# A hybrid decoder layer on one core: raw branch gates passed through the sigmoid at the merge, attention results loaded ahead, a new split of the fillers

## The chip, the cores and the metric

The kernel runs on one core of a Trainium2 chip. A core has a matrix engine (PE, which loads weights beside its matmuls, PEld), a vector engine (DVE), an activation engine (ACT), a general engine (POOL) and a queue engine (SP), which here issues all transfers between device memory and the on-chip buffers. Each engine works through its own instructions in order and waits for the others by semaphores. The metric is device time in microseconds, the median of several executions. Trace times are counted from the start of the profiled execution.

## The reference

One layer over 1024 positions of width 1024, in float32:

```
proj = rmsnorm(x) @ w_in        -> attention q,k,v, short-conv B,C,v, DeltaNet q,k,v,
                                   beta, decay, output gate z, and 3 x 1024 branch gates
A: forgetting attention (causal, 8 heads)                  -> y_fox
B: y_sc = B * causal_dwconv3(C * v)
C: gated delta rule in chunks, per-head RMSNorm * silu(z)  -> y_dn
merged = sum_b sigmoid(gate_b) * (y_b @ W_branch_b)
x = x + merged @ w_o
x = x + (silu(u_gate) * u_val) @ w_down   with u = causal_dwconv3(rmsnorm(x) @ w_up)
x = x + sigmoid(rmsnorm(x) @ w_pg) * (p @ w_ple)
```

The reference's delta rule has chunks of 64; the kernel works on 8 chunks of 128 with 4 heads side by side. In each chunk a lower triangular matrix A is built from k, beta and the decay, its inverse is formed, and a recursion over the chunks carries a state.

## The kernel before

Activations lie transposed, 128 channels by 1024 positions; `NB` are the two halves of 512 positions. Every float32 matmul is made of three: `split` (L127 to L130) writes a rounded high part on ACT (L129) and the rest as a low part on DVE or POOL (L130), and `step` multiplies high by high, high by low and low by high. A unit of the first projection is 128 output channels: 2 halves x 8 x 3 = 48 matmuls of 128x512 (`dense`). The normalised input is held in 16 tiles xg (8 high, 8 low), which the first projection reads until its last unit and which later operands reuse. Weights come in tiles wr of 512 KB and are split into wo.

Stages in order of time: the first norm and attention with projections in between (to about 522 us); phase f2, the delta rule, in two parts: the solve (`dn_solve`: building A, inverting 32x32 blocks on DVE, completing them to 128x128 on PE) and the steps (`dn_prep`, `dn_state`, `dn_out` for 8 chunks); then phase la with the gates, the merge, w_o, the channel mixer and the last projection.

The units of the first projection that nothing needs at once are fillers for PE. There are 32 of them: 12 for the short convolution, 4 for z, and 16 raw gates of branches 0 and 2 (the gates of branch 1 are made later, in phase la). `PLAN` says how many are started at which point of attention, solve and steps; a filler's result goes unscaled to device memory (`raw_tile`, L503 and L504, 64 stores of 256 KB). Within the plan the order of all instructions on each engine is set by the scheduler, which runs a timeline of its own.

In the solve, `decay` loads per chunk a row tile gb (256 KB, L703), DVE makes et of it (4 instructions, L705), ACT the exponential; a tile kc (256 KB, L717) is multiplied by itself on PE, and DVE writes A (L722). gb and kc have 2 buffers each. With all eight chunks of A, DVE transposes (L728), does the forward substitution in 31 rounds (L734, L736), and transposes back to TT (L739) and X (L748); then PE's first product with X (`to64`) can start. The recursion's tail is `dn_out` of the last chunk: products into po, squares on ACT, small steps on DVE, a scaling (L859), and transposes on PE (L862).

In phase la, eight units make the gates of branch 1, each followed by `gate` for two tiles of a raw gate (branches 0 and 2): load from device memory, product with the norm's scale rs on DVE (`mul`, L950), sigmoid on ACT (L986), store (L987). Four short convolutions (`short_conv`) and four output gatings (`dn_gated`) on DVE and ACT follow units 0 to 3 and 4 to 7; each keeps 1024 positions in tiles yr (4 buffers) and stores its y. At the merge, per branch, four y tiles are loaded (`load`, into yr), split into xg, and eight units of 24 matmuls are multiplied by the gates, which come back through tiles sg (4 buffers). Branch 0 writes `merged`, 1 and 2 add to it on POOL (L1021).

Of the kernel before, what the change touches and what calls it, by code (L numbers as in the profile page):

```python
# [7 lines left out]
F32 = mybir.dt.float32  # L8
# [5 lines left out]
P = 128  # L14
# [13 lines left out]
WR, WO, SUMS, SUBS = 2, 5, "gvgv", "vvvvvvg"  # L28
PLAIN = 2
MM, PQ, SM1, SM2 = 2, 2, 2, 4  # L30
PLAN = {"start": "krr", "tail": "rr", "solve": "rrrrrrrrrrr",
        "steps": ["rr", "rr", "r", "r", "r", "r", "r", "rr", "r"],
        "fox": [["", "", "", "v"],
                ["k", "v", "", ""],
                ["", "", "", "r"],
# [13 lines left out]
def hybrid_block(ctx: ExitStack, tc: tile.TileContext, I, out, dbg=None):  # L49
# [33 lines left out]
    def pt(tag, bufs, w=512, dt=F32):  # L83
        pool, n = homes.setdefault(tag, (scopes[-1], bufs))
        return pool.tile([P, w], dt, tag=tag, name=nm(tag), bufs=n)
# [14 lines left out]
    def tmp(role="tmp", dt=F32, w=512):  # L100
        return pt(role if role in homes else "tmp", 0, 516, dt)[:, 0:w]
# [597 lines left out]

    def decay(c, mask, op, sign):  # L700

        gb, e = pt("gb", 2), pt("et", 2)
        Q.dma_start(chunk(gb), cdr[8:12, hs(c)].partition_broadcast(P))  # L703
        for h in range(4):
            V.scalar_tensor_tensor(out=e[:, hs(h)], in0=gb[:, hs(h)], scalar=Gc[:, h, c : c + 1], in1=mask,  # L705
                                   op0=ALU.subtract, op1=op)
        S.activation(e, e, AF.Exp, scale=sign)
        return gb, e

    def dn_solve():  # L710
# [2 lines left out]
            G.memset(TT[:, 4 * c : 4 * c + 4, :], 0.0)  # L713
        for c in range(8):
            _, ee = decay(c, maskS, ALU.max, -1.0)
            kc = pt("kc", 2)
            Q.dma_start(chunk(kc), kdr[:, :, hs(c)])  # L717
            ps = smb()
            for h in range(4):
                mm(ps[:, hs(h)], kc[:, hs(h)], kc[:, hs(h)], True, True)  # L720
            for h in range(4):
                V.scalar_tensor_tensor(out=A[:, 4 * c + h, :], in0=ps[:, hs(h)], scalar=beta[:, h, c : c + 1],  # L722
                                       in1=ee[:, hs(h)], op0=ALU.mult, op1=ALU.mult)
# [220 lines left out]
    with phase("la", psum=dict(mm=6, sm=2), a=16, wq=3):  # L944
        with phase("me", tmp=9, sg=4, yr=4):
# [3 lines left out]
            def mul(o, x, y):  # L949
                V.tensor_tensor(out=o, in0=x, in1=y, op=ALU.mult)  # L950
# [27 lines left out]
                mul(y, y, z)  # L978
                Q.dma_start(ydr[2][j], y)

            def gate(b, dt, nb, ps):
                g = tmp()
                if ps is None:
                    Q.dma_start(g, raw[U_GT + 8 * b + dt][:, NB[nb]])
                mul(g, g if ps is None else ps, rs[:, NB[nb]])
                S.activation(g, g, AF.Sigmoid)  # L986
                Q.dma_start(gdr[b, dt][:, NB[nb]], g)  # L987

            for b in range(3):
                for dt in range(8):  # L990
                    gdr[b, dt] = dr.tile([P, T], F32, tag=f"g{b}{dt}", name=f"g{b}{dt}")
            for dt in range(8):
                dense(wload(I["win"][U_GT + 8 + dt]), KT, xg, lambda nb, ps, dt=dt: gate(1, dt, nb, ps))
                for i in range(2):
                    for nb in range(2):
                        gate(2 * (dt // 4), 2 * (dt % 4) + i, nb, None)
                (short_conv, dn_gated)[dt // 4](dt % 4)

            merged = [big() for _ in range(8)]
            for b in range(3):  # L1000
                ys = []
                for j in range(4):
                    y, h, l = load(ydr[b][j]), xgt(), xgt()
                    split(h, l, y)
                    ys.append((h, l))
                for d2 in range(4):
                    sgs = {}
                    for dt in (2 * d2, 2 * d2 + 1):
                        for nb in range(2):
                            sgs[dt, nb] = pt("sg", 4)  # L1010
                            Q.dma_start(sgs[dt, nb], gdr[b, dt][:, NB[nb]])
                    w = wload(I["wbr"][4 * b + d2])
                    for dt in (2 * d2, 2 * d2 + 1):
                        def ev_b(nb, ps, dt=dt):
# [243 lines left out]
```

## Time and profile before

| what | value |
|---|---|
| median of three executions | 2026.06 us (2025.57 to 2030.67) |
| the profiled execution, its time | 2031.17 us |
| its span in the trace | 2029.4 us |
| PE busy | 1946.1 us, 96% |
| DVE, ACT, POOL busy | 1336.6, 906.9, 534.5 us |
| mean granted clock of PE | 0.985 |
| moved by transfers | 236.2 MB, mean 116 GB/s |

The page's second part cuts the span into 40 slices of 50.7 us; a digit is the busy share in tenths. The queries of waits give for each pair of waiting line and releasing line the sum, the number of times and the longest wait. A row of stretches gives the busy time of each engine, the granted clock, the share in which the DMA engines were busy, and GB/s. In rows of groups the idle time stands after the bar, with what ended it. On PE the durations of single matmuls overlap, so the pace is read from how many start in a stretch.

### The profile page before, as it was taken

What the parts mean: (1) busy time and instruction counts of PE and PEld (TensorE: products, weight loads), DVE (VectorE), ACT (ScalarE), POOL (GpSimd) and SP (SyncE); (2) the same over time, 40 slices, a digit from 0 to 9 for tenths busy, and PEclk for the clock granted to TensorE, in tenths of its full rate; (3) what the DMA queues carried; (4) which work ended last, traced back from release to release, by engine and by line L of the source; (5) the groups of instructions that cost most, each with busy time, mean ns of one, the idle gap of its engine ahead of it and who ended that gap; (6) DMA issues with size and microseconds to landing.
All of it is one profiled execution on the core that took longest, in us unless ns stands there. A gap on an engine that the chain in (4) does not pass through costs nothing. (4 is left out here: it accounts for less than half of the span.)

```text
span 2029.4 us, 25549 instructions
## 1 busy us (share of the span) xinstructions
PE 1946.1 (96%) x9281; PEld 1616.4 (80%) x9281; DVE 1336.6 (66%) x2157; ACT 906.9 (45%) x1651; POOL 534.5 (26%) x435
## 2 busy tenths in 40 slices
PE   8999999999997999999499999999999999999998
PEld 6788888888786888878388887787777778888887
DVE  6888788888396123348654537888788788544564
ACT  6576877677221233334421325544444444212351
POOL 1545334434322221200015310234334341000210
PEclk9999999999998999999699999999999999999999
DMA  4221122122431334259964523112221216432132
GB/s 174 69 97 58 57 68 80 47 82 77 146 101 51 99 122 131 90 206 395 366 220 136 191 96 123 62 52 83 73 94 63 94 63 237 137 94 73 52 109 89
DMA packets 111854, 236.20 MB, mean 116 GB/s; under 512 B 10384, under 2 KB 41456, under 8 KB 111728
## 3 DMA queue, kind: packets, MB, share of 16 engines
q1 hardware_dynamic: 111728, 234.57, 33.8%
q8 instruction: 73, 1.20, 0.2%
q14 instruction: 53, 0.43, 0.1%
HBM read 167.37 MB, written 67.16 MB: 116 GB/s over the span
## 5 line engine op out<-in xcount | busy, mean ns | idle before, releaser
L126 PE MATMUL mm<-xg,wo 128*128 128x512 f32 x6128 | 1493.6, 395 | 44.8 <-ACT xg L129 28.8
L126 PEld LDWEIGHTS mm<-xg,wo 128*128 128x128 f32 x6128 | 1146.4, 189 | 288.3 <-ACT xg L129 29.2
L126 PE MATMUL mm<-a,wo 128*128 128x512 f32 x1216 | 304.1, 390 | 0.3 <-ACT u L227 0.3
L129 ACT ACTIVATE wo<-wr 128x512 fp32r<-128x512 f32 x232 | 144.7, 626 | 292.8 <-PE mm L126 284.5
L126 PEld LDWEIGHTS mm<-a,wo 128*128 128x128 f32 x1216 | 229.0, 188 | 48.2 <-ACT u L227 0.7
L130 POOL TENSOR_TENSOR wo<-wr,wo 128x512 fp32r<-128x512 f32 x108 | 152.1, 1410 | 356.9 <-ACT wo L129 349.1
L1160 DVE TENSOR_TENSOR a<-mm,a 128x512 f32<-128x512 f32 x96 | 65.3, 690 | 92.1 <-PE mm L126 91.9
L130 DVE TENSOR_TENSOR wo<-wr,wo 128x512 fp32r<-128x512 f32 x124 | 96.2, 777 | 40.4 <-ACT wo L129 40.1
L1021 POOL TENSOR_TENSOR a<-a,sg 128x512 f32<-128x512 f32 x32 | 50.3, 1574 | 232.2 <-DMA sg<-g 197.3
L280 POOL TENSOR_TENSOR tmp<-tmp,tmp 128x512 f32<-128x512 f32 x21 | 27.7, 1323 | 286.9 <-ACT tmp L278 285.0
L130 DVE TENSOR_TENSOR wo<-wq,wo 128x512 fp32r<-128x512 f32 x68 | 79.2, 1166 | 3.4 <-ACT wo L129 3.4
L1073 DVE SCALAR_TENSOR_TENSOR o<-cw,cols,o 128x1024 f32<-128x1024 f32 x44 | 77.8, 1768 | 0.0
L491 DVE SCALAR_TENSOR_TENSOR o<-cv,cols,o 128x512 f32<-128x512 f32 x72 | 69.9, 971 | 10.1 <-ACT o L489 9.1
L129 ACT ACTIVATE wo<-ws 128x512 fp32r<-128x512 f32 x80 | 50.2, 631 | 56.5 <-PE mm L126 54.8
L503 ACT ACTIVATE o<-mm 128x512 f32<-128x512 f32 x60 | 35.7, 594 | 88.7 <-PE mm L126 70.4
L600 ACT ACTIVATE pp<-pp,small 128x512 f32<-128x512 f32 (+2 forms) x96 | 58.4, 610 | 27.9 <-DVE small L594 27.5
L1105 POOL TENSOR_TENSOR cg<-o,cg 128x1024 f32<-128x1024 f32 x22 | 55.0, 2501 | 48.1 <-ACT cg L1104 48.1
L199 POOL TENSOR_TENSOR ws<-wq 128x512 f32<-128x512 f32 x20 | 27.8, 1392 | 120.1 <-DMA wq<-wup 87.4
L130 DVE TENSOR_TENSOR pl<-pq,ph 128x512 fp32r<-128x512 f32 (+1 forms) x80 | 49.9, 629 | 13.9 <-ACT ph L129 13.5
L1071 ACT ACTIVATE o<-cw,cols 128x1024 f32<-128x1024 f32 x22 | 25.4, 1156 | 75.1 <-DVE cw L223 75.1
L199 POOL TENSOR_TENSOR ws<-wq,wq 128x512 f32<-128x512 f32 x20 | 43.7, 2184 | 56.3 <-DVE wo L130 52.3
L1073 DVE SCALAR_TENSOR_TENSOR o<-cg,cols,o 128x1024 f32<-128x1024 f32 x44 | 57.2, 1301 | 0.8 <-ACT o L1071 0.7
(289 smaller groups left out, 2407.2 us busy)
## 6 DMA issues: line engine op xcount, KB each, us to landing
wr<-win SPq DMA_DIRECT2D x64, 512.0 KB, 3.5
wq<-wup SPq DMA_DIRECT2D x44, 512.0 KB, 3.5
r<-o SPq DMA_DIRECT2D x64, 256.0 KB, 2.5
g<-tmp SPq DMA_DIRECT2D x48, 256.0 KB, 6.0
sg<-g SPq DMA_DIRECT2D x48, 256.0 KB, 2.9
ad<-o SPq DMA_DIRECT2D x20, 512.0 KB, 3.8
wq<-ad SPq DMA_DIRECT2D x20, 512.0 KB, 4.6
wr<-wdn SPq DMA_DIRECT2D x20, 512.0 KB, 3.6
```

Of the source, the lines that this page charges most:

```text
L126: pe[0] = nc.tensor.matmul(o, lhsT=l, rhs=r, start=start, stop=stop, skip_group_check=more)
L129: S.activation(h, x, AF.Copy)
L130: (eng or V).tensor_tensor(out=l, in0=x, in1=h.bitcast(F32), op=ALU.subtract)
L199: (G if e == "g" else V).tensor_tensor(out=o, in0=x, in1=y, op=op)
L280: eng[nb].tensor_tensor(out=acc[nb], in0=acc[nb], in1=sq, op=ALU.add)
L491: V.scalar_tensor_tensor(out=o, in0=cv[:, i : i + 512], scalar=col(c0 + i), in1=o, op0=ALU.mult, op1=ALU.add)
L503: S.activation(o, ps, AF.Copy)
L600: S.activation(t[:, :w], t[:, :w], AF.Exp, bias=mn[:, k - 1 : k], scale=-1.0, accum_out=sm[:, i : i + 1])
L1021: G.tensor_tensor(out=m, in0=m, in1=t, op=ALU.add)
L1073: V.scalar_tensor_tensor(out=o, in0=cv[:, i : i + T], scalar=col(c0 + i), in1=o, op0=ALU.mult, op1=ALU.add)
L1105: G.tensor_tensor(out=sg, in0=o, in1=sg, op=ALU.mult)
L1160: V.tensor_tensor(out=x2[dt][:, NB[nb]], in0=ps, in1=x2[dt][:, NB[nb]], op=ALU.add)
```

## The change

Six things are different.

- `PLAN`: the solve starts 13 fillers instead of 11; the steps start 2, 1, 1, 1, 1, 1, 1, 1, 1 instead of 2, 2, 1, 1, 1, 1, 1, 2, 1 (at the ninth point no filler is left, before as now).
- gb has 3 buffers instead of 2.
- kc has 4 buffers instead of 2.
- The raw gates of branches 0 and 2 no longer pass through device memory a second time. `gate` and its 32 loads and 32 stores are gone; the merge loads the raw gate into sg, multiplies it by rs on DVE and applies the sigmoid on ACT there. The gates of branch 1 are made as before.
- The four attention results are loaded at the start of phase la into four tiles of their own (fox), not at the merge into yr.
- The list of scaled gates in device memory shrinks from 24 to 8.

```diff
-PLAN = {"start": "krr", "tail": "rr", "solve": "rrrrrrrrrrr",
-        "steps": ["rr", "rr", "r", "r", "r", "r", "r", "rr", "r"],
+PLAN = {"start": "krr", "tail": "rr", "solve": "rrrrrrrrrrrrr",
+        "steps": ["rr", "r", "r", "r", "r", "r", "r", "r", "r"],
...
-        gb, e = pt("gb", 2), pt("et", 2)
+        gb, e = pt("gb", 3), pt("et", 2)
...
-            kc = pt("kc", 2)
+            kc = pt("kc", 4)
...
-            def gate(b, dt, nb, ps):
-                g = tmp()
-                if ps is None:
-                    Q.dma_start(g, raw[U_GT + 8 * b + dt][:, NB[nb]])
-                mul(g, g if ps is None else ps, rs[:, NB[nb]])
-                S.activation(g, g, AF.Sigmoid)
-                Q.dma_start(gdr[b, dt][:, NB[nb]], g)
-
-            for b in range(3):
-                for dt in range(8):
-                    gdr[b, dt] = dr.tile([P, T], F32, tag=f"g{b}{dt}", name=f"g{b}{dt}")
+            fox = [big() for _ in range(4)]
+            for j in range(4):
+                Q.dma_start(fox[j], ydr[0][j])
             for dt in range(8):
-                dense(wload(I["win"][U_GT + 8 + dt]), KT, xg, lambda nb, ps, dt=dt: gate(1, dt, nb, ps))
-                for i in range(2):
-                    for nb in range(2):
-                        gate(2 * (dt // 4), 2 * (dt % 4) + i, nb, None)
+                gdr[dt] = dr.tile([P, T], F32, tag=f"g{dt}", name=f"g{dt}")
+
+                def ev_g(nb, ps, dt=dt):
+                    g = tmp()
+                    mul(g, ps, rs[:, NB[nb]])
+                    S.activation(g, g, AF.Sigmoid)
+                    Q.dma_start(gdr[dt][:, NB[nb]], g)
+                dense(wload(I["win"][U_GT + 8 + dt]), KT, xg, ev_g)
                 (short_conv, dn_gated)[dt // 4](dt % 4)
...
-                    y, h, l = load(ydr[b][j]), xgt(), xgt()
+                    y, h, l = load(ydr[b][j]) if b else fox[j], xgt(), xgt()
...
-                            sgs[dt, nb] = pt("sg", 4)
-                            Q.dma_start(sgs[dt, nb], gdr[b, dt][:, NB[nb]])
+                            g = sgs[dt, nb] = pt("sg", 4)
+                            Q.dma_start(g, (gdr[dt] if b == 1 else raw[U_GT + 8 * b + dt])[:, NB[nb]])
+                            if b != 1:
+                                mul(g, g, rs[:, NB[nb]])
+                                S.activation(g, g, AF.Sigmoid)
```

The scheduler then orders the engines anew from the solve on. Three places matter. Names are those of the code, with numbers that tell tiles apart; L is the line, and the waits name the semaphores that an instruction waits for.

SP's queue in the building of A, before: the third gb waits for DVE, and the third and fourth kc wait for PE.

```order
L703 DMA gb_5646<-cdr 128x4x128 [waits DMAHW1_49]
L717 DMA kc_5654<-kdr 128x4x128 [waits DMAHW2_49,PE_49]
L703 DMA gb_5665<-cdr 128x4x128 [waits DMAHW6_49,DMAHW3_49,DVE_49]
L504 DMA r_6204<-o_6238 128x512 [waits DMAHW4_49,Activation_49]
L703 DMA gb_5684<-cdr 128x4x128 [waits DMAHW5_49,DMAHW1_49,DVE_49]
L717 DMA kc_5673<-kdr 128x4x128 [waits DMAHW7_49,PE_49]
L717 DMA kc_5692<-kdr 128x4x128 [waits DMAHW2_49,PE_49]
```

The same place now:

```order
L703 DMA gb_5646<-cdr 128x4x128 [waits DMAHW1_49]
L717 DMA kc_5654<-kdr 128x4x128 [waits DMAHW2_49]
L703 DMA gb_5665<-cdr 128x4x128 [waits DMAHW3_49]
L717 DMA kc_5673<-kdr 128x4x128 [waits DMAHW4_49]
L717 DMA kc_5692<-kdr 128x4x128 [waits DMAHW5_49]
L703 DMA gb_5684<-cdr 128x4x128 [waits DMAHW6_49,DVE_49]
L504 DMA r_6204<-o_6238 128x512 [waits DMAHW7_49,Activation_49]
```

The third gb and two more kc now follow at once; the fourth gb is the first that waits for DVE.

PE where the solve's first products with X stand (sm from X and A; mm are a filler's matmuls). This piece of the difference is from the stretch after the forward substitution:

```order
 L126 MATMUL mm_6668<-xg_245,wo_6665 128x512
+L126 MATMUL sm_5907<-X_5899,A_1235_5905 128x128 x4
+L126 MATMUL sm_5914<-sw_5897,TT_5618 128x128 x4
+L126 MATMUL sm_5915<-TT_5618,sw_5897 128x128 x4
 L126 MATMUL mm_6668<-xg_258,wo_6665 128x512
 L126 MATMUL mm_6668<-xg_259,wo_6665 128x512
-L126 MATMUL sm_5892<-X_5884,A_1231_5890 128x128 x4
```

The first product with X (sm_5892) has left this place for one 30 filler matmuls earlier, and the products of the second chunk stand where it was.

DVE where the merge begins, before (xg from yr: the attention results' low parts):

```order
L950 TENSOR_TENSOR tmp_9303<-tmp_9303,rs_427 128x512 [waits DMAHW4_49,DMAHW0_49]
L950 TENSOR_TENSOR tmp_9308<-tmp_9308,rs_427 128x512 [waits DMAHW7_49,DMAHW3_49]
L950 TENSOR_TENSOR tmp_9313<-tmp_9313,rs_427 128x512 [waits DMAHW6_49,DMAHW1_49]
L950 TENSOR_TENSOR tmp_9318<-tmp_9318,rs_427 128x512 [waits DMAHW3_49,DMAHW0_49]
L950 TENSOR_TENSOR yr_9323<-yr_9323,rs_427 128x1024 [waits DMAHW4_49]
L950 TENSOR_TENSOR yr_9323<-yr_9323,yr_9327 128x1024 [waits Activation_49]
L950 TENSOR_TENSOR yr_9325<-yr_9325,yr_9323 128x1024 [waits DMAHW5_49,DVE_49]
L130 TENSOR_TENSOR xg_9344<-yr_9341,xg_9343 128x1024 [waits DMAHW3_49,Activation_49]
```

And now (xg from a: the tiles loaded ahead):

```order
L130 TENSOR_TENSOR xg_9174<-a_8513,xg_9173 128x1024 [waits PE_49,Activation_49]
L950 TENSOR_TENSOR yr_9155<-yr_9155,rs_427 128x1024 [waits DMAHW6_49,DMAHW1_49]
L130 TENSOR_TENSOR xg_9178<-a_8514,xg_9177 128x1024 [waits PE_49,Activation_49]
L130 TENSOR_TENSOR wo_9290<-wr_9285,wo_9290 128x512 [waits Activation_49]
L130 TENSOR_TENSOR xg_9182<-a_8515,xg_9181 128x1024 [waits Activation_49]
L950 TENSOR_TENSOR tmp_9151<-mm_9126,rs_427 128x512 [waits PE_49]
L950 TENSOR_TENSOR yr_9155<-yr_9155,yr_9159 128x1024 [waits Activation_49]
L130 TENSOR_TENSOR xg_9186<-a_8516,xg_9185 128x1024 [waits Activation_49]
```

Before, the four splits came after all gate products and the last output gating and waited for transfers of their own; now they wait for PE and ACT alone, mixed with the last output gating (yr_9155), whose load DVE waits for between the first split and the second.

## The prediction

> **What bounds the kernel now.** I read the page's busy line and slices first, then what PE waited for, then the stretches around those waits.
>
> ```profile
> span 2029.4 us, 25549 instructions
> PE 1946.1 (96%) x9281; PEld 1616.4 (80%) x9281; DVE 1336.6 (66%) x2157; ACT 906.9 (45%) x1651; POOL 534.5 (26%) x435
> PE   8999999999997999999499999999999999999998
> DMA  4221122122431334259964523112221216432132
> ```
>
> PE is busy for 96%, and its matrix work is the same before and after. So the change can only win back what PE loses: 83 us of idle time and the slow clock that follows an idle time. The slices show two dents, at 610 us and at 965 to 1015 us; at the second the DMA engines are full. PE's waits name them:
>
> ```profile
> PE mm L126 <- ACT xg L129: 28.8, 1, 28.8
> PE sm L126 <- DVE X L748: 11.3, 1, 11.3
> PE po L862 <- DVE yr L959: 3.8, 1, 3.8
> PE sm L126 <- DVE et L705: 3.8, 1, 3.8
> ```
>
> 28.8 us at the start of the merge (the attention result's high half is late), 11.3 us in the solve (the first transposed inverse X is late), 3.8 us at the tail of the recursion and 3.8 us in the building of A. Each costs more than its wait, since the clock falls (columns: stretch, PE, PEld, DVE, ACT, POOL busy us, granted clock, DMA share, GB/s):
>
> ```profile
> 885.00:890.00 5.00, 4.02 (x12) 3.38 (x13) 0.81 (x3) 1.97 (x2) 0.00 (x0) 0.50 0.19 56
> 890.00:895.00 5.00, 5.00 (x20) 4.02 (x19) 0.00 (x0) 0.00 (x0) 0.00 (x0) 0.81 0.73 243
> 985.00:995.00 10.00, 0.00 (x0) 0.00 (x0) 6.27 (x8) 3.94 (x7) 0.00 (x0) 0.50 1.04 411
> 1050.00:1100.00 50.00, 50.00 (x222) 41.45 (x221) 22.74 (x31) 9.30 (x13) 25.69 (x17) 1.00 0.52 166
> 886.72 89.74 PE L126 MATMUL mm<-xg,wo 128*128 128x512 f32 x384
> 1005.22 55.08 PE L126 MATMUL mm<-xg,wo 128*128 128x512 f32 x229 [28.76 <-ACT xg L129]
> ```
>
> At full clock 222 matmuls take 50 us, 0.2252 us each. The 229 after the long wait took 55.1 instead of 51.6: 3.5 us lost. The 384 of the gates, after the wait of 3.8 us, took 89.7 instead of 86.5: 3.3 us lost. The clock there was granted at 0.50.
>
> **The merge.** Why is the attention result late? Its loads stand at the end of SP's queue, behind everything that the gates send:
>
> ```profile
> DMA packets 18511, 43.82 MB, mean 371 GB/s; under 512 B 2005, under 2 KB 2517, under 8 KB 18504
> g<-tmp SPq DMA_DIRECT2D x48, 256.0 KB, 6.0
> tmp<-r SPq DMA_DIRECT2D x32, 256.0 KB, 6.2
> L950 DVE TENSOR_TENSOR tmp<-tmp,rs 128x512 f32<-128x512 f32 x32 | 21.2, 686 | 4.1 <-DMA tmp<-r 4.1
> L950 DVE TENSOR_TENSOR yr<-yr,yr 128x1024 f32<-128x1024 f32 x16 | 19.6, 1222 | 13.2 <-DMA yr<-r 10.8 <-ACT yr L976 2.2
> L950 DVE TENSOR_TENSOR yr<-yr,rs 128x1024 f32<-128x1024 f32 x16 | 19.6, 1222 | 1.2 <-DMA yr<-r 1.0
> L130 DVE TENSOR_TENSOR wo<-wr,wo 128x512 fp32r<-128x512 f32 x16 | 11.0, 688 | 7.2 <-ACT wo L129 7.1
> L950 DVE TENSOR_TENSOR tmp<-mm,rs 128x512 f32<-128x512 f32 x16 | 10.8, 684 | 0.0
> L966 DVE SCALAR_TENSOR_TENSOR yr<-yr,cols,yr 128x1024 f32<-128x1024 f32 x8 | 10.2, 1280 | 2.6 <-ACT yr L964 2.6
> 895.47 1.23 DVE L950 TENSOR_TENSOR yr<-yr,yr 128x1024 f32<-128x1024 f32 x1 [9.63 <-DMA yr<-r]
> ```
>
> These rows cover 887 to 1005 us. 43.8 MB at 371 GB/s are 118 us, while PE needs 89.7. The change takes out 32 loads (tmp<-r) and 32 of the 48 stores (g<-tmp), 64 x 0.262 = 16.8 MB. 27 MB remain, 73 us at the same rate, less than PE's 89.7. DMA no longer sets the end.
>
> DVE is the next candidate. Its rows add to 92.4 us; the four splits of the attention result (1.22 each) make it 97.3; 28 of the 32 products leave the stretch (the four of the first merge group are now done in it): 97.3 - 28 x 0.686 = 78.1 us. Before, DVE's large work began 8.7 us after PE's (895.47 against 886.72). The four new loads stand ahead of the first convolution's, 2.1 MB at 371 GB/s, 5.7 us: it begins at 14.4, and is through at 14.4 + 78.1 = 92.5 us if it never waits. PE ends the gates at 89.7, and its first 40 products (9.0 us) are ordered so that the last low half is needed only at 98.7. So DVE may lose 6.2 us to late loads and sigmoids before PE waits for the last split. The first split can't start before the last gate group frees xg, 21 matmuls or 4.7 us before its end. I take 2 us of remaining waits, between 0 (DVE never late) and 12 (DVE loses as much as the idle times in the rows above come to without the first 9.6 us: 4.1 + 3.6 + 1.2 + 7.2 + 2.6 = 18.7, less the 6.2), nearer to none because those waits came from loads of 6 us in a full queue and from ACT waiting on PE. Term: -28.8 - 3.5 + 2.0 = **-30.3 us**, bounds -32.3 and -17 (12 us with the clock's loss).
>
> The 28 remaining products (0.686 us on DVE) and sigmoids (0.63 us on ACT) move into the merge, where DVE has room: in 1050 to 1100 us, quoted above, it works 22.7 of 50 us; 16 products in the 43 us of one branch add 11. What could bind is the round of an sg buffer:
>
> ```profile
> L1021 POOL TENSOR_TENSOR a<-a,sg 128x512 f32<-128x512 f32 x32 | 50.3, 1574 | 232.2 <-DMA sg<-g 197.3 <-DVE sg L1020 34.9
> L1020 DVE TENSOR_TENSOR sg<-mm,sg 128x512 f32<-128x512 f32 x21 | 14.5, 691 | 28.6 <-PE mm L126 28.5
> sg<-g SPq DMA_DIRECT2D x48, 256.0 KB, 2.9
> L986 ACT ACTIVATE tmp<-tmp 128x512 f32<-128x512 f32 x48 | 29.6, 630 | 46.7 <-DVE tmp L950 44.2 <-issue 1.4 <-DMA g<-tmp 1.1
> ```
>
> Eviction 0.69, POOL's sum 1.57, load 2.9, product 0.69, sigmoid 0.63: 6.5 us, with five hand-overs about 7.5 us. PE takes four groups of 12 matmuls in that round, 10.8 us. Term: 0.
>
> The Trainium skill (SBUF — State Buffer, section on the two separate sides) says that VectorE with two SBUF inputs and GpSimd lock each other out of a shared port pair for a whole instruction. The new products have two SBUF inputs and stand beside POOL's sums in the third branch. POOL's subtraction of 128x512 takes 1.41 us elsewhere and this sum 1.57, which shows no such loss. By the rule the round grows by at most one product and one sum, to 9.8 us: still under 10.8, the sum unchanged, but it raises the chance of the slow rival below from 2 to 4 in 100.
>
> **The solve.** The third buffer for gb and the fourth for kc let loads run ahead while A is built:
>
> ```profile
> 526.92 0.42 SPq L703 DMA_DIRECT2D gb<-cdr  x1
> 532.05 0.37 SPq L703 DMA_DIRECT2D gb<-cdr  x1
> DMA to landing us min/median/max: 4.8/5.9/8.3
> 530.88 1.14 DVE L705 SCALAR_TENSOR_TENSOR et<-gb,gall,cst 128x128 f32<-128x128 f32 x4 [6.47 <-DMA gb<-cdr]
> 563.08 2.16 DVE L722 SCALAR_TENSOR_TENSOR A<-sm,beta,et 128x128 f32<-128x128 f32 x8 [2.15 <-PE sm L126]
> 628.39 9.06 DVE L748 STREAM_TRANSPOSE X<-TT 32x128 f32<-32x128 f32 x32
> 631.66 2.08 PE L126 MATMUL sm<-X,A 128*128 128x128 f32 x8 [11.31 <-DVE X L748]
> ```
>
> Now the third gb goes out at about 528, and each later one only needs the product (L705) three before it: issues at 532.1, 535.2, 538.1 (behind a weight load), 540.9 and 542.4 (before, the third waited for its buffer until 532.05, just after the first L705 had ended). With the median landing of 5.9 us the last is there at 548.3; the products and the exponential in the order of the new program end at 553.3 instead of 565.2. The chain from there to X has nothing but DVE in it, so X is ready 11.9 us earlier, at 619.8. With landings of 8.3 us it is 9 us, with 4.8 us 14; if the transfers and not the buffers set the pace, nothing.
>
> But PE does not use the wait better. By the order, 369 filler matmuls stood between the last attention product and the first product with X; now there are 339, for the scheduler expects X sooner than the chip has it. The two added fillers come behind the solve. PE reaches X at 620.35 - 3.8 - 3.3 - 30 x 0.2252 = 606.5 and waits some 13 us, again with the clock's loss. What counts is the end: X comes 11.9 us earlier, and 30 more matmuls (6.8 us) follow it. Term: -11.9 + 6.8 = **-5.1 us**, bounds -7 and +6.8. The 3.8 us wait of the building is inside this term.
>
> **The steps and their tail.** 528 fillers lay between the first preparation and the end of the recursion, now 432 (of 1069 in all, as before). One step's chain is short: three products, w, vn and the state's update, which is four instructions like w's.
>
> ```profile
> 852.60 1.05 PE L126 MATMUL sm<-S,ks 128*128 128x128 f32 x8
> 853.69 1.13 DVE L825 SCALAR_TENSOR_TENSOR w<-sm,nbe,bv 128x128 f32<-128x128 f32 x4 [0.44 <-PE sm L126]
> 857.55 0.58 ACT L831 ACTIVATE vn<-sm 128x512 f32<-128x512 f32 x1
> 861.38 0.69 DVE L813 TENSOR_TENSOR pd<-ev,et 128x512 f32<-128x512 f32 x1 [1.45 <-PE ev L126]
> 885.98 1.08 PE L862 MATMUL po<-cst,on 128*128 128x128 f32 x4 [3.77 <-DVE yr L959]
> ```
>
> 3 x 1.05 + 2 x 1.13 + 0.58 = 6.0, some 7 us with hand-overs, against 48 fillers a step, 10.8 us: no new wait. The tail is barer: 95 fillers stood between the last product with X and the last output, now 10. So PE waits for pd (0.69 and a hand-over of 0.2) ahead of the last output, then 3.8 us as before. Term: **+0.9 us**, bounds 0 and 4.
>
> **Sum:** -30.3 - 5.1 + 0.9 = -34.5 us against the profiled execution, 2031.17 us with a span of 2029.4. The median shown, 2026.06, is 5.1 us below that execution; I take the difference over to it: 1991.6, so 1991.
>
> **Rivals.** (1) DVE takes DMA's place at the merge: it loses 18.7 us and PE waits 12 instead of 2, then runs 3.5 us slow: 1991 + 10 + 3.5 = 2004. For it: 78 of 90 us, and a start 14 us late; against it: the 6.2 us of slack and a queue that is no longer full. (2) The building of A is paced by its transfers, not by buffers: +6.8 instead of -5.1, 2003. For it: landings up to 8.3 us; against it: the issue at 532.05, 5.1 us after the one before. (3) The long wait does not go, since the attention result was not what PE lacked, but xg or an entry of DVE that stands ahead: only the solve's and the tail's terms, 2022. Against it: the DMA share of 1.04. (4) Slower: the round of sg in the first and third branches exceeds 10.8 us. There are seven refills of four, so each us above costs 7; it decides from 10.8 + 34.5/7 = 15.7 us on. At 18 us: 7 x 7.2 = 50, 2042. It needs landings of 13 us instead of 2.9.
>
> **How the numbers follow.** Forecast 63 in 100, (1) 18, (2) 11, (3) 4, (4) 4. The forecast's bounds are 1985 (no wait left, A 2 us earlier still) and 1998; (1) and (2) reach 2004, both together 2016. Range 1984 to 2006. Faster by over 0.3% (6 us, about what this kernel's runs can tell from no change): forecast, (1), (2): 0.92; within: (3), 0.04; slower: (4), 0.04.
>
> **What would show it.** The wait of PE for ACT xg under 6 us and DMA share under 0.9 in the gates' stretch; 64 fewer issues on SP; the wait for et L705 gone; X's first product near 620 us after a wait of 11 to 15 us; a tail wait still there. A wait for X below 8 us, a merge wait above 8, or waits of PE for sg in the merge would prove a step wrong.

## The result and the profile after

The changed kernel takes 2004.91 us, the median of four executions (2003.33 to 2006.48), against 2028.28 us for the kernel before, four executions in the same session (2025.57 to 2030.67). The ratio is 0.9885, with a 95% interval of 0.9867 to 0.9904. The profiled execution took 2005.48 us with a span of 2003.7 us: 25.7 us less than the profiled execution of before, where the prediction's sum was 34.5.

First the page of the changed kernel: the slices of PE and of the DMA engines, and the bytes moved.

```profile
PE   8999999999997999999999999999999999999998
DMA  4221112122521334447853423112222226332132
DMA packets 102636, 219.40 MB, mean 109 GB/s; under 512 B 9360, under 2 KB 40432, under 8 KB 102512
```

PE's second dent, at 965 to 1015 us, is gone; the first, at 610 us, is still there. The bytes fell by 16.8 MB, the 64 transfers of 0.262 MB that the change takes out. In the slices of the gates the DMA digits are 7 and 8 where they were 9 and 9.

Then what PE waited for (sum, times, longest, in us):

```profile
PE sm L126 <- DVE X L748: 12.2, 1, 12.2
PE sm L126 <- DMA kc<-kdr: 4.0, 4, 2.2
PE po L862 <- DVE yr L959: 3.8, 1, 3.8
PE mm L126 <- ACT a L129: 3.1, 2, 2.5
PE mm L126 <- DVE xg L130: 0.9, 1, 0.9
```

The wait of 28.8 us for the attention result doesn't exist any more. The wait for X is 0.9 us longer than before. The waits of the building of A are now for kc, a transfer. New are the last two rows: the splits of the merged result, which the output product w_o reads.

Where the time went is read from PE's timeline (start, duration, line, operation, count, in brackets the idle time ahead and what ended it). Before:

```profile
521.72 0.44 PE L126 MATMUL py<-pl,st 128*128 128x128 f32 x2
1138.79 0.39 PE L126 MATMUL mm<-a,wo 128*128 128x512 f32 x1
1251.30 8.91 PE L126 MATMUL mm<-xg,wo 128*128 128x512 f32 x38 [1.65 <-ACT wo L129]
```

After:

```profile
521.39 0.44 PE L126 MATMUL py<-pl,st 128*128 128x128 f32 x2
623.51 2.07 PE L126 MATMUL sm<-X,A 128*128 128x128 f32 x8 [12.18 <-DVE X L748]
886.05 219.89 PE L126 MATMUL mm<-xg,wo 128*128 128x512 f32 x960
1105.78 0.39 PE L126 MATMUL mm<-a,wo 128*128 128x512 f32 x1
1115.64 1.22 PE L126 MATMUL mm<-a,wo 128*128 128x512 f32 x2 [2.46 <-ACT a L129]
1225.08 35.20 PE L126 MATMUL mm<-xg,wo 128*128 128x512 f32 x154 [1.65 <-ACT wo L129]
```

The first row of each is the last attention product. The last row is the same place in both kernels, behind w_o; call it the late mark. Four stretches:

| stretch | before, us | after, us | difference |
|---|---|---|---|
| last attention product to X's first product | 109.94 | 102.12 | -7.8 |
| X's first product to the gates' first | 255.06 | 262.54 | +7.5 |
| gates' first product to the late mark | 364.58 | 339.03 | -25.6 |
| late mark to the end | 778.1 | 778.6 | +0.5 |

The start of the span adds -0.3. So the solve won 7.8 us and gave 7.5 back before the gates, and the whole gain is in the gates and the merge. There 960 matmuls follow each other without a wait, 219.9 us where full speed (0.2252 us each, from the prediction) is 216.2. From before's 364.58, the long wait (28.76) and its slow clock (3.5) leave 332.3; the changed kernel needs 339.0. The missing 6.7 us are lost just behind the merge:

```profile
1110.00:1120.00 10.00, 6.00 (x16) 4.12 (x16) 8.17 (x11) 6.61 (x10) 4.08 (x3) 0.66 0.64 232
```

In these 10 us PE started 16 matmuls instead of 44: 4.0 us of waits, the rest at a granted clock that averaged 0.66. DVE is the engine that is late. Its evictions of the third branch (L1019 in the new line numbers, 16 of them; first and last), after and then before:

```profile
1066.86 0.68 DVE L1019 TENSOR_TENSOR sg<-mm,sg 128x512 f32<-128x512 f32 x1
1113.72 0.68 DVE L1019 TENSOR_TENSOR sg<-mm,sg 128x512 f32<-128x512 f32 x1
```

```profile
1098.25 0.69 DVE L1020 TENSOR_TENSOR sg<-mm,sg 128x512 f32<-128x512 f32 x1 [1.42 <-PE mm L126]
1138.99 0.69 DVE L1020 TENSOR_TENSOR sg<-mm,sg 128x512 f32<-128x512 f32 x1 [1.18 <-PE mm L126]
```

After, 15 intervals take 46.86 us, 3.12 each; before, 40.74 us, 2.72 each, which is PE's own pace of 12 matmuls. DVE falls 15 x 0.4 = 6 us behind. PE doesn't notice during the branch, because six PSUM banks take up the lag. It notices at w_o, whose first group of products needs the splits of all merged tiles, one after the other: the last eviction starts 7.9 us after PE has gone on to w_o at 1105.78, and before the change 0.2 us after. From w_o's first product to the late mark PE needs 119.3 us, before 112.5.

### The profile page after: what moved, and what is told of

Its sections match the earlier page's. It is cut to its first block, busy times and chain, and to the rows that moved or that the text cites. A ratio compares the mean times of both kernels' runs of the same rounds, so it can differ in the third digit from the quotient of the medians.

```text
span 2003.7 us, 25407 instructions
## 1 busy us (share of the span) xinstructions
PE 1943.1 (97%) x9281; PEld 1611.3 (80%) x9281; DVE 1338.9 (67%) x2157; ACT 908.0 (45%) x1651; POOL 531.3 (27%) x435
## 5 line engine op out<-in xcount | busy, mean ns | idle before, releaser
L126 PE MATMUL mm<-xg,wo 128*128 128x512 f32 x6128 | 1488.0, 393 | 17.7 <-DVE wo L130 12.2
L130 DVE TENSOR_TENSOR wo<-wr,wo 128x512 fp32r<-128x512 f32 x124 | 89.6, 724 | 27.4 <-ACT wo L129 26.8
L130 DVE TENSOR_TENSOR pl<-pq,ph 128x512 fp32r<-128x512 f32 (+1 forms) x80 | 49.9, 629 | 13.9 <-ACT ph L129 13.5
L199 DVE TENSOR_TENSOR ws<-ws,wq 128x512 f32<-128x512 f32 x20 | 14.9, 745 | 64.2 <-POOL ws L199 64.2
```

The lines of the kernel that those rows point to most:

```text
L126: pe[0] = nc.tensor.matmul(o, lhsT=l, rhs=r, start=start, stop=stop, skip_group_check=more)
L130: (eng or V).tensor_tensor(out=l, in0=x, in1=h.bitcast(F32), op=ALU.subtract)
L199: (G if e == "g" else V).tensor_tensor(out=o, in0=x, in1=y, op=op)
```

## Experiments

Each kernel is the changed kernel with one edit unless it says otherwise. Times are medians; each ratio is to the kernel before, run in the same session. The changed kernel ran in its own session only, and before's median moved between 2028.3 and 2031.0 us from one session to another, so differences of 3 us from 2004.9 decide nothing; the readings rest on the traces. "Gates to mark" is the third stretch of the table above. All compute the whole layer.

### What removed the wait at the merge: the move or the early loads

Only the early loads kept; the raw gates pass through device memory a second time, as before:

```
-    g = tmp(); mul(g, ps, rs...); sigmoid; store        (branch 1)
+    gate(1, ...) and, after each unit, two tiles of gate(0 or 2, ...): load, mul, sigmoid, store
-    merge: load raw gate, mul, sigmoid
+    merge: load finished gate
```

> Undone: the move of the raw gates; all 48 gate groups are again loaded, scaled, passed through the sigmoid and stored while the gates' products run. Kept: the early loads of the attention result, the buffers, the fillers. Theory A (what was late before was the attention result alone, since its loads stood last in SP's queue): PE has no wait at the start of the merge although the DMA engines are as full as before (43.8 MB, share near 1); and since the third branch has no products on VectorE again, the wait at the start of the output product goes too (4.0 us and about 3 us of slow clock): 1996 to 2000 us, under the changed kernel's 2005. Rival B (it was the volume: 43.8 MB need 118 us, PE 90): something else is late, PE waits 12 to 29 us at the start of the merge or for sg in it: 2012 to 2030.

Measured: 2014.97 us (2012.91 to 2018.94), 0.9935 (0.9920 to 0.9951). Gates to mark: 348.8 us.

```profile
1029.74 0.79 SPq L954 DMA_DIRECT2D yr<-y  x2
1035.40 1.06 ACT L129 ACTIVATE xg<-yr 128x1024 fp32r<-128x1024 f32 x1 [7.02 <-DMA yr<-y]
1036.51 13.74 PE L126 MATMUL mm<-xg,wo 128*128 128x512 f32 x48 [13.25 <-ACT xg L129]
```

Rival B. The first branch starts without a wait, but the second doesn't: the loads of its y tiles go out at 1029.74, behind the gates' transfers in SP's queue, and PE waits 13.25 us for their split. With the DMA engines as full as before (share 0.99 from 890 to 980 us) the early loads only pass the wait on to the next branch. Nothing is lost at w_o in this kernel, whose third branch has no products on DVE.

Only the move kept; the attention result is loaded at the merge:

```
-    fox = [big() for _ in range(4)]; 4 loads ahead of the gates
-    y = load(ydr[b][j]) if b else fox[j]
+    y = load(ydr[b][j])
```

> Undone: the early loads of the attention result; they stand again behind the gates' stretch in SP's queue. Kept: the raw gates' move, the buffers, the fillers. Theory A (place in the queue): the loads go out only when a yr buffer comes free from the last normalised outputs, near the end of the gates' products; PE waits 5 to 15 us at the start of the merge, then runs 3 us slow: 2010 to 2022. Rival B (volume: with 27 MB instead of 43.8 the queue is through before PE): no wait, 2003 to 2007, as the changed kernel.

Measured: 2014.56 us (2014.33 to 2018.08), 0.9935 (0.9920 to 0.9950). Gates to mark: 346.3 us.

```profile
980.35 3.11 PE L126 MATMUL mm<-xg,wo 128*128 128x512 f32 x7 [3.71 <-ACT xg L129]
```

Theory A in time, with a wait shorter than expected: 3.7 us at the merge instead of 5 to 15. The move alone takes some 25 of the 28.8 us; the early loads take the rest, its slow clock and 1 us more at w_o (346.27 - 339.03 = 7.2 us). Up to w_o's first product, the early loads alone win 15.8 us against before, the move alone 26.0, both 32.3: the two overlap. So the volume in the queue was the larger cause, the place in the queue the smaller, and only both together leave no wait.

### What is given back at w_o

Order of the branches:

```
-            for b in range(3):
+            for b in (0, 2, 1):
```

> The merge takes its branches in the order 0, 2, 1 instead of 0, 1, 2; nothing else. Theory A (in the changed kernel the third branch's evictions come every 3.12 us against PE's 2.70, because its gates are scaled on VectorE there; 15 x 0.42 = 6.3 us of lag, hidden by the six PSUM banks, show at the start of the output product as 4.0 us of waits and about 3 us of slow clock): with those gates in the middle branch the lag is worked off in the last one, whose gates come finished; no wait at the start of the output product: 1996 to 2000. Rival B (the lag belongs to the last branch whatever its gates, since the sums and the splits of the merged result crowd there): the waits stay, 2003 to 2007. Rival C: the recurrence's outputs are needed 43 us earlier and are late: a new wait, over 2007.

Measured: 2003.80 us (2002.11 to 2006.11), 0.9879 (0.9864 to 0.9893). Gates to mark: 334.4 us, 4.6 less than the changed kernel.

```profile
1068.09 41.48 PE L126 MATMUL mm<-xg,wo 128*128 128x512 f32 x180 [0.36 <-DVE sg L1019]
1113.01 0.68 DVE L1019 TENSOR_TENSOR sg<-mm,sg 128x512 f32<-128x512 f32 x1
```

The lag moves with those gates: now PE waits 0.36 us for an eviction at the end of the middle branch, when the banks are full. In the last branch DVE catches up, though not wholly; its last eviction starts 3.6 us after PE has gone on to w_o (1109.41), and PE still waits 0.6 us there. Theory A in the trace: from w_o's first product to the mark PE needs 113.4 us instead of 119.3. The time misses A's 1996 to 2000 and lies in B's range; this profiled execution reached its gates at 888.46, 2.4 us later than the changed kernel, in a part that the edit doesn't touch.

More buffers:

```
-        with phase("me", tmp=9, sg=4, yr=4):
+        with phase("me", tmp=7, sg=6, yr=4):
```

> Six sg buffers instead of four; for the space, seven tmp buffers instead of nine. Theory A1 (the lag in the third branch is latency: the round of a buffer, load, product, sigmoid, eviction, sum, is 12.5 us where PE takes four groups in 10.8): with six buffers a round of 12.5 us is under six groups, 16.2 us; the wait at the start of the output product goes: 1996 to 2001. Rival A2 (VectorE's own pace: its products are held up beside POOL's sums, 1.78 us instead of 0.68, and stand ahead of the evictions): the evictions still come every 3.0 us or slower and the wait stays: 2003 to 2007. With fewer tmp buffers a wait in the gates or at the second norm may rise by some us.

Measured: 2005.54 us (2003.11 to 2007.49), 0.9890 (0.9873 to 0.9906). Gates to mark: 335.9 us.

```profile
1066.08 0.68 DVE L1019 TENSOR_TENSOR sg<-mm,sg 128x512 f32<-128x512 f32 x1
1110.38 0.68 DVE L1019 TENSOR_TENSOR sg<-mm,sg 128x512 f32<-128x512 f32 x1
1112.29 1.22 PE L126 MATMUL mm<-a,wo 128*128 128x512 f32 x2 [2.85 <-ACT a L129]
```

The pace is 44.30 / 15 = 2.95 us, and the wait at w_o stays: from w_o's first product to the mark 118.2 us, against 119.3. The other 2.0 us of the shorter stretch lie at the start of the gates, where the clock stayed at 1.00 after the tail's wait (885 to 890 us; 0.50 in the changed kernel); nothing ties that to the buffers. Nearer to A2: buffers are the smaller part of the lag. The run also has two tmp buffers fewer, which may hide some of their effect.

Scaling where the raw gate is written, so that the products leave the merge while the late loads and sigmoids stay:

```
 def f(nb, ps):                                   # eviction of a raw unit
     o = tmp("o")
-    S.activation(o, ps, AF.Copy)
+    if u < U_GT: S.activation(o, ps, AF.Copy)
+    else: V.tensor_tensor(out=o, in0=ps, in1=rs[:, NB[nb]], op=ALU.mult)
 ...
-    mul(g, g, rs[:, NB[nb]])                     # in the merge
     S.activation(g, g, AF.Sigmoid)
```

> The raw gates are scaled where they are written: their eviction in the recursion is a product on VectorE (0.69 us) in place of a copy on ScalarE (0.60), and the 32 products leave the merge, where only the sigmoid stays. Theory A (the third branch lags because of its products on VectorE, held up by the loads and by POOL's sums): evictions there every 2.7 us as before the change, no wait at the start of the output product, 4 us of idle time and some 3 us of slow clock less: 1997 to 2001. Rival A2 (the late gates themselves, load and sigmoid with four buffers, make the lag): evictions still at 3.0 us or slower, waits of 3 to 4 us stay: 2003 to 2007. Rival B (VectorE is the bound of the solve): evictions that fall between the building and X delay X by 0.7 us each; X's first product over 625 us.

Measured: 2000.48 us (1999.12 to 2000.93), 0.9858 (0.9844 to 0.9873). Gates to mark: 331.8 us, 7.2 less than the changed kernel.

```profile
1065.48 0.69 DVE L1021 TENSOR_TENSOR sg<-mm,sg 128x512 f32<-128x512 f32 x1
1106.21 0.69 DVE L1021 TENSOR_TENSOR sg<-mm,sg 128x512 f32<-128x512 f32 x1 [0.92 <-PE mm L126]
630.24 4.42 PE L126 MATMUL mm<-xg,wo 128*128 128x512 f32 x18 [1.44 <-DVE o L506]
```

Theory A: the pace is 40.73 / 15 = 2.72 us again, DVE waits for PE and not PE for DVE, and the wait at w_o is gone. The products on DVE made the lag: in the five kernels here without them in the third branch PE needs 112.5 us from w_o's first product to the mark, in the seven with them there and four buffers 119.2 to 120.3. The last row is a price that the expectation didn't have: in the solve PE waits 1.4 us for a scaled eviction, L506.

### The solve

The buffers undone:

```
-        gb, e = pt("gb", 3), pt("et", 2)      kc = pt("kc", 4)
+        gb, e = pt("gb", 2), pt("et", 2)      kc = pt("kc", 2)
```

> Undone: the buffers; gb and kc have two again. Kept: the rest of the change. Theory A (the buffers bring X 8.2 us earlier, but PE then has 30 fillers, 6.8 us, after X that stood before it): X's first product back near 631.5 us after a wait of 11 to 12 us, the gates' first product within 2 us of the changed kernel's 886.05, the time 2004 to 2008. Rival B (the buffers' gain reaches the end and was lost elsewhere): gates' first product 5 us or more later than 886.05, the time 2010 or more.

Measured: 2008.35 us (one execution). 

```profile
629.76 2.07 PE L126 MATMUL sm<-X,A 128*128 128x128 f32 x8 [11.30 <-DVE X L748]
886.39 13.88 PE L126 MATMUL mm<-xg,wo 128*128 128x512 f32 x56
```

X 6.3 us later, the gates 0.3 us later: theory A by the trace (the time lies just over its range). With the old buffers the scheduler puts the 30 fillers back ahead of X: 369 filler matmuls stand there, as before the change, against 339. The eight kernels with the new buffers and 339 fillers take 102.1 to 105.1 us from the last attention product to X's first one (mean 103.5), the two with the old buffers and 369 fillers 109.3 and 109.9; PE waits for X in all ten. The buffers bring X 6.1 us earlier, and the 30 fillers behind X (6.8 us) return it.

The table of fillers undone:

```
-        "solve": "rrrrrrrrrrrrr", "steps": ["rr", "r", "r", "r", "r", "r", "r", "r", "r"]
+        "solve": "rrrrrrrrrrr",   "steps": ["rr", "rr", "r", "r", "r", "r", "r", "rr", "r"]
```

> Undone: the table of fillers; 11 in the solve and two in the second and eighth step, as before. Kept: the rest of the change. Theory A (the order up to the recursion doesn't depend on it: as many fillers before X and as many behind it): X's first product near 623.5 us after 12.2 us of wait, gates' first product within 1 us of 886.05, the time 2003 to 2007. Rival B (the table moved the fillers that X lacks): X's wait under 9 us and the time under 2002.

Measured: 2004.45 us (one execution).

```profile
623.46 2.08 PE L126 MATMUL sm<-X,A 128*128 128x128 f32 x8 [12.17 <-DVE X L748]
```

Theory A: X as in the changed kernel, and the gates' first product at 885.9 against 886.1. The part of the change that is in its name, two more fillers, neither wins nor costs anything that shows.

Loads of two chunks at a time while A is built, in pieces of 1 KB instead of 512 bytes:

```
+            if c % 2 == 0:
+                two = slice(c * P, c * P + 2 * P)
+                Q.dma_start(g2, cdr[8:12, two].partition_broadcast(P))
+                Q.dma_start(k2, kdr[:, :, two])
```

> While A is built, the loads of the decays and of the keys take two chunks at a time: 8 loads of 512 KB in pieces of 1 KB instead of 16 of 256 KB in pieces of 512 bytes; the same bytes, two buffers of two chunks for each. Theory A (the building is paced by these loads, and their small pieces make them slow: 168 GB/s at a DMA share of some 0.8): the last product of the building ends at 551 to 553 us instead of 556.2, X's first product comes 3 to 5 us earlier (618.5 to 620.5), its wait falls from 12.2 to 7 to 9, the time to 2000 to 2002. Rival B (latency or bytes, not the pieces; the first pair also lands later than a first single chunk): X no earlier than 623, the time 2004 to 2008.

Measured: 2002.84 us (2001.19 to 2003.60), 0.9862 (0.9844 to 0.9881). The transfers of the changed kernel in the building (count, KB each, median us to landing), then of this one:

```profile
gb<-cdr SPq DMA_DIRECT2D x8, 256.0 KB, 6.8
kc<-kdr SPq DMA_DIRECT2D x8, 256.0 KB, 7.4
```

```profile
gb<-cdr SPq DMA_DIRECT2D x4, 512.0 KB, 6.9
kc<-kdr SPq DMA_DIRECT2D x4, 512.0 KB, 7.5
```

```profile
551.00 2.15 DVE L731 SCALAR_TENSOR_TENSOR A<-sm,beta,et 128x128 f32<-128x128 f32 x8
620.32 2.08 PE L126 MATMUL sm<-X,A 128*128 128x128 f32 x8 [11.95 <-DVE X L757]
881.80 18.45 PE L126 MATMUL mm<-xg,wo 128*128 128x512 f32 x73
```

Twice the bytes land in the same time; the number of loads is halved along with the doubled pieces, so which of the two helps isn't told apart. The building ends at 553.2 instead of 556.2 and X's product comes at 620.3, as theory A has it. Its forecast of a shorter wait for X was wrong: PE, which waits less for kc (2.3 us instead of 4.0), reaches the same filler earlier too. The gates start 4.2 us earlier; the times' intervals overlap with the changed kernel's.

The first product with X behind 8 of the 13 fillers:

```
+        filler(PLAN["early"], 0)                 # 8 of the solve's 13, ahead of the first to64
+        with tc.issue_after(pe[0].ins):          # around to64's first product with X
```

> The first product with X is ordered behind 8 of the solve's 13 fillers: 397 filler matmuls stand between the last attention product and it instead of 339, and 55 fewer behind it. Theory A (X's wait costs only because too few fillers stand before it; in the recursion they cover nothing that would wait): 58 x 0.2252 = 13.1 us more work fills the wait of 12.2, the 3.3 us of slow clock go with it: 1989 to 1993. Rival B (the recursion or its tail needs them): new waits of PE for w, S, vn or po of 5 us and more: 1995 to 2005.

Measured: 1990.66 us (1989.37 to 1996.49), 0.9808 (0.9788 to 0.9829).

```profile
624.20 1.05 PE L126 MATMUL sm<-X,A 128*128 128x128 f32 x8
871.25 4.12 PE L126 MATMUL mm<-xg,wo 128*128 128x512 f32 x10
```

Theory A: X is no earlier, nothing waits for it, and the gates start 14.8 us earlier. The recursion doesn't miss the fillers. So with the order fixed, X may be ready whenever it likes up to 624 us; the buffers of the change work on a quantity that the order of the fillers decides.

The last filler behind the last output's first products:

```
+                    if c == 8: mark()
-                    filler(PLAN["steps"][c], 1)      # "steps": 8th "r"
+                    filler(PLAN["steps"][c], c < 8)  # "steps": 8th ""
```

> The last filler, 48 products, is ordered behind the last output's first products instead of in the eighth step. Theory A (the 3.8 us wait before the last output's transposition is a matter of order alone; the clock's loss of 3.3 us goes with it): no wait there, 2004.9 - 7 = 1998, 1996 to 2000. Rival B (the wait moves: w, vn or pd is late in the eighth step, or a wait stays since the gates' weights come later): 2002 to 2007.

Measured: 2001.36 us (1999.50 to 2004.37), 0.9865 (0.9850 to 0.9880).

```profile
625.99 2.07 PE L126 MATMUL sm<-X,A 128*128 128x128 f32 x8 [12.18 <-DVE X L748]
875.09 0.46 PE L126 MATMUL po<-S,qe 128*128 128x128 f32 x2 [0.87 <-ACT yo L864]
1225.56 34.77 PE L126 MATMUL mm<-xg,wo 128*128 128x512 f32 x152 [1.65 <-ACT wo L129]
```

The wait of 3.8 us is gone, but from X's first product to the late mark only 2.0 us are won (599.6 against 601.6), not 7: the eighth step, now without a filler, waits 0.9 us for the output tile yo and 1.1 us for bv. Between A and B.

### Combinations

All four improvements (the scaling, the pairs, the early fillers, the tail):

> Together: the first product with X behind 8 fillers, loads of two chunks while A is built, gates scaled where they are written, the last filler behind the last output's first products. If the terms add: 2004.9 - 14.3 (first product with X) - 1.5 (what is left of the building's waits) - 5 (start of the output product) - 7 (tail) = 1977, 1973 to 1984. If the fillers taken from the recursion are now missed there (59 + 48 of 634 gone), new waits of PE for w, vn or S: 1984 to 1992.

Measured: 2000.32 us (1999.26 to 2000.73), 0.9857 (0.9841 to 0.9874). Both halves of the expectation missed; the terms neither add nor is the loss in the recursion.

```profile
626.83 1.65 PE L126 MATMUL mm<-xg,wo 128*128 128x512 f32 x3 [16.16 <-DVE o L506]
617.47 8.58 DVE L760 STREAM_TRANSPOSE X<-TT 32x128 f32<-32x128 f32 x31
626.08 0.69 DVE L506 TENSOR_TENSOR o<-mm,rs 128x512 f32<-128x512 f32 x1
```

The last fillers ahead of X are raw gates. With the scaling their evictions are on DVE, and they stand behind the substitution and the transposes in DVE's order. Their PSUM banks (fillers have two) stay full, and PE waits 16.2 us for a bank ahead of X instead of for X. The next run puts these evictions back on ACT as copies, and the wait is gone.

The scaling at the write only for branch 2, whose fillers run in the recursion; pairs and early fillers as above; the tail left alone:

```
-            if u < U_GT: S.activation(o, ps, AF.Copy)
+            if u < U_GT + 16: S.activation(o, ps, AF.Copy)
```

> Together, with the collision of the previous combination taken out: the first product with X behind 8 fillers, loads of two chunks while A is built, and the scaling at the write only for the third branch's gates, whose fillers run in the recursion and not beside the solve's long run on VectorE; the first branch's raw gates are copied by ScalarE and scaled in the merge, as in the changed kernel; the tail as in it. Theory (the 16.2 us wait was the 8th filler's bank held by an eviction queued behind the substitution on VectorE): no wait for o in the solve, none for X, none at the start of the output product: 1990.7 - 7 (start of the output product) - 2 (waits of the building) = 1982, 1978 to 1986. Rival (the evictions on VectorE delay the recursion's chain where 55 fillers are gone): waits of PE for w, S or vn, 1986 to 1993.

Measured: 1980.47 us (1979.57 to 1984.75), 0.9759 (0.9745 to 0.9774).

```profile
866.24 219.98 PE L126 MATMUL mm<-xg,wo 128*128 128x512 f32 x960
1198.55 48.37 PE L126 MATMUL mm<-xg,wo 128*128 128x512 f32 x212 [1.64 <-ACT wo L129]
```

The waits for X, for o and at w_o are gone, and of those for kc 1.5 us are left; the gates start at 866.2 and need 332.3 us to the mark, just what is left of before's 364.6 without its long wait. This version is 24 us faster than the changed kernel by the medians of two sessions (before's median was 2.7 us higher in this one).

## Why the prediction was right, and where it was off

The direction, the main mechanism and the range held; the size didn't: 1991 was predicted, 2004.9 measured. Of the 13.9 us, 8.8 are terms of the sum (34.5 predicted, 25.7 between the two profiled executions). The rest lies in the base: the two medians are 23.4 us apart, 2.3 less than the profiled executions, the median of before was 2.2 us higher with the fourth execution, and 0.6 is rounding. The range held by 1.1 us, and that is partly luck: the forecast's own bounds, 1985 to 1998, were missed, and the room above them was made for the rivals (1) and (2). Of these (1) did not happen and (2) did by half; the rest of the room was used up by a term that stood at nothing.

**The merge** (-30.3 predicted, -25.6 measured). The first half was right and on the careful side: PE has no wait at all at the start of the merge, where 2 us were allowed for. Its cause was named as the queue with 43.8 MB in it; the two half-changes bear that out, with the volume as the larger part. Up to w_o's first product the stretch is 32.3 us shorter; 6.8 us are given back behind it.

**The round of sg, "Term: 0"**, is the step that failed. It was added up from durations and hand-overs to 7.5 us and compared with PE's 10.8. Measured, a buffer of the third branch comes round in 4 x 3.12 = 12.5 us. The slow rival (4) had this mechanism and a chance of 4 in 100, but a price in the wrong place: PE doesn't stall at the refills, since six PSUM banks lie between, and all of it falls due at w_o: 4.0 us of waits and 2.7 us of slow clock. The sum asked whether one buffer comes round in time, not what DVE has to do in the third branch in all. There the next gate's product stands ahead of an eviction that is ready, and waits for its load; and a product beside a POOL sum is slow. Both show in two rows of groups, first in the first branch (no work on POOL) and then in the third, with one product and one sum of the third behind them:

```profile
L950 DVE TENSOR_TENSOR sg<-sg,rs 128x512 f32<-128x512 f32 x12 | 8.3, 690 | 4.3 <-DMA sg<-r 4.2
L950 DVE TENSOR_TENSOR sg<-sg,rs 128x512 f32<-128x512 f32 x15 | 15.1, 1006 | 9.7 <-DMA sg<-r 9.7
1094.56 1.78 DVE L950 TENSOR_TENSOR sg<-sg,rs 128x512 f32<-128x512 f32 x1
1094.18 1.61 POOL L1020 TENSOR_TENSOR a<-a,sg 128x512 f32<-128x512 f32 x1 [2.50 <-DVE sg L1019]
```

The product takes 0.69 us in the first branch and 1.01 us on the mean in the third: ten of the 15 take 0.68 or 0.69 us, and the five that start inside a sum end 0.55 us after that sum. The eviction, which reads PSUM and one tile of SBUF, keeps its 0.68 us, also the three times that it starts inside a sum. The Trainium skill (SBUF — State Buffer, section on the two separate sides) says that a VectorE instruction with two SBUF inputs and a GpSimd one that reads SBUF exclude each other for a whole instruction, and these rows agree.

The prediction looked for this in a mean of POOL's durations and read 1.57 as no loss. That mean hid it: in the changed kernel's third branch a sum takes 1.27 to 1.30 us alone and 1.60 to 1.67 where such an operation of DVE is running as it starts. And before's own trace shows it on DVE, whose split of the weights (also two tiles of SBUF) meets a sum there again and again, with 1.78 us instead of 0.69:

```profile
1128.95 1.68 POOL L1021 TENSOR_TENSOR a<-a,sg 128x512 f32<-128x512 f32 x1 [0.87 <-DVE sg L1020]
1129.39 1.78 DVE L130 TENSOR_TENSOR wo<-wr,wo 128x512 fp32r<-128x512 f32 x1
```

So these collisions are not new, and they alone make no lag. From the first to the last eviction of the third branch:

| in us | before | changed | scaled at the write |
|---|---|---|---|
| DVE's operations with two SBUF inputs, time beyond 0.69 each | 7.6 | 7.7 | 8.7 |
| the gates' products on DVE | none | 13 | none |
| DVE waits for loads of sg | 0 | 7.0 | 0 |
| DVE waits for ACT | 0 | 1.9 | 3.7 |
| DVE waits for PE | 11.8 | 0 | 5.6 |

The collisions are spread over more operations, but their sum stays. What the change adds is 13 products (0.60 us each from start to start without a collision, 7.8 us) and 7.0 us of waiting for their loads, against 11.8 us that DVE had to spare. The prediction's allowance of one product and one sum, 9.8 us of round against the 12.5 measured, left these out. That the products cause the lag is shown by the run that takes them out. How it divides between their own time and the loads that they wait for is worked out here, not tried by a run; six buffers recover only 0.17 of the 0.4 us per group.

**The solve** (-5.1 predicted, -0.3 measured together with the tail, whose +0.9 was right in kind: PE waits 0.6 us for pd, and 3.8 us as before). The structure was right: X comes earlier, 30 more fillers behind it take the gain away, and the wait for X stays (13 predicted, 12.2 measured). The term that was mis-sized is the 11.9 us for X, which measured 7.8 in these two profiles and 6.1 over all kernels. The landing times were taken from before, 5.9 us at the median; with more loads in flight they became 6.8 for gb and 7.4 for kc, and PE waited for kc; with the old buffers back they are 6.0 and 5.3. That is the mechanism of rival (2), transfers that set the pace, at about half its strength; the run with pairs, whose building ends 3.0 us earlier, bears it out.

**What would show it.** Four of the five signs came as written: no wait for the attention result and a DMA share of 0.83 in the gates' stretch, 64 fewer transfers, no wait for et, the tail's wait in its place. X's first product came at 623.5 instead of near 620. The list had a sign for waits for sg, and none for the start of w_o, where the loss turned up.

## What to carry to other kernels

A stage that runs slower than the matmuls behind deep PSUM buffering shows no wait where it is slow; its lag is paid at the next point that needs all of its results, so compare the pace of evictions with PE's, first to last, and add up all that the evicting engine does there in its order, waits included, not the round of one buffer. Before work is moved to an engine, read what stands ahead of it in that engine's order at its new place: the same scaled eviction was free in the recursion and cost 16 us beside the substitution. And where PE waits for a chain that it could cover, moving independent work ahead of the wait (14.8 us here) can be worth far more than shortening the chain (0.3 us).

## What the runs showed of the hardware

- An elementwise operation with both inputs in SBUF took 0.69 us on DVE alone; started inside a POOL sum of the same size it ended 0.54 to 0.56 us after the sum (up to 1.78 us in all). POOL's sum in the changed kernel's third branch took 1.60 to 1.67 us instead of 1.27 to 1.30 when one was running as it started. A product with an input in PSUM kept 0.68.
- A wait mostly costs PE more than its length. Filling the 12.2 us wait for X brought the gates 14.8 us forward; the 4.0 us of waits at w_o cost 6.7. The addition isn't fixed: after the same wait of 3.78 us at the tail PE started 13 matmuls from 885 to 890 us at a granted clock of 0.50 in the changed kernel, and 22 at 1.00 in the one with six sg buffers.
- Loads of 512 KB in pieces of 1 KB landed as fast (6.9 and 7.5 us) as loads of 256 KB in pieces of 512 bytes (6.8 and 7.4).
- Kernels with the same order of the solve differed by up to 3 us from one profile to another in the time from the last attention product to X; differences below that need the mean of several.
